# Gate stores from SyncE's queue in quarters, maxima in quarters, and two idle buffers for the first expert table

## The chip, the core and the metric

One core of one Trainium2 chip runs the whole program. The metric is the device time of one execution in microseconds (us). TensorE (PE) does the matmuls, VectorE (DVE) and ScalarE (ACT) the elementwise work, GpSimd (POOL) issues the gathers that go by an index list, and SyncE (SP) issues the plain loads. DMAs can be issued by SP, ACT and POOL, each on a queue of its own.

## The reference, cut to what matters

Two transformer blocks in float32 run one after the other on 256 tokens of width 2048. The change lies in the last part of the first block, a mixture over 16,384 experts, of which each token takes 16 in each of 8 heads:

```python
def peer(x, w_pq, sub_k1, sub_k2, u_emb, v_emb):     # T = 256 tokens, D = 2048
    q = (xt @ w_pq).reshape(T, 8, 2, 128)
    s1, s2 = ...                                     # scores against 2 x 128 keys per head
    v1, i1 = lax.top_k(s1, 16); v2, i2 = lax.top_k(s2, 16)
    cand = v1[..., :, None] + v2[..., None, :]       # 256 pairs, expert = i1 * 128 + i2
    sc, sel = lax.top_k(cand, 16)
    gates = jax.nn.softmax(sc, axis=-1)
    act = jax.nn.gelu(xt . u_emb[expert])            # first expert table, 128 MB
    return sum over experts of gate * act * v_emb[expert]   # second expert table
```

## The kernel before, in words

**Dense first table.** The kernel doesn't gather rows of `u_emb`. It computes the activation of every token with every expert as a dense product (stage u, line 777 on): 32 column blocks, each of four weight tiles of 128x2048 floats (1 MB), so 128 tiles. Stage v (line 798 on) then takes only those rows of `v_emb` that some token uses.

**A weight tile.** `linear` (138) calls `wtile` (108): SP loads a tile into `raw`, a pool of three buffers (112), line 113. `halves` (116) cuts it in two halves of 1024 columns; for each, ACT rounds the values into `whi` (123) and DVE subtracts to get the rest, `wlo` (124). Each of these has four buffers of half a tile. PE multiplies three times for each 128x512 piece: high by high (134), high by low (135), low by high (136), in all 24 matmuls of 512 columns for a tile. A tile's buffer is free for the next load when DVE has made the second `wlo` of it.

**Block end of stage u.** ACT applies gelu (783), PE transposes (790), ACT copies to `actT` (792), and ACT's queue stores it to the DRAM array AG (794).

**Routing beside it.** At a lower priority the scheduler puts the routing between the work of stage u. The gates (lines 651 to 682) come in four sets of 64 tokens. For each token a one-hot matmul (667) gives its gates for all 128x128 experts. ACT copies the high part out (672), and DVE adds the low part and puts the sum into `gsb` (673), an array of 128x128x64 floats of which there is one buffer. At the end of a set, ACT's queue stores `gsb` to AG in two halves of 2 MB (676), and DVE takes the maximum over the 64 tokens in one instruction (678 for even sets, 681 for odd ones). After the fourth set, lines 684 to 774 find out which experts are used, and build lists of them: sixteen groups of three DVE instructions (743, 745, 749) and eight matmuls (752), which end in `idv` (758) and `idg` (762). With `idv` POOL gathers rows of `v_emb` (130, into `raw` and `vraw`), with `idg` it gathers gates and activations from AG (130, into `vag`); `vh` (824) is their product, `vhh` and `vhl` (826, 828) its two parts, and stage v multiplies them by the rows.

**Order.** The tile framework's scheduler writes the order on each engine ahead of time, by priorities and its own simulated timeline. An instruction on an engine, and a DMA in an engine's queue, does not start before the ones that stand ahead of it there.

Of the kernel before, what the change touches and what calls it, by code (L numbers as in the profile page):

```python
# [12 lines left out]
F32 = mybir.dt.float32  # L13
# [5 lines left out]
ALU = mybir.AluOpType  # L19
AX = mybir.AxisListType  # L20

P = 128
# [34 lines left out]
def tile_kernel(ctx: ExitStack, tc: tile.TileContext, A, out):  # L57
    nc = tc.nc
    V, S, G, TE = nc.vector, nc.scalar, nc.gpsimd, nc.tensor

    def pool(name, bufs=1, space=None, stack=ctx):
        kw = {"space": space} if space is not None else {}
        return stack.enter_context(tc.tile_pool(name=name, bufs=bufs, **kw))
# [8 lines left out]
    def bank(name="bk"):  # L72
        tg, nb = {"lin": ("lin", 3), "tp": ("tp", 2), "sc": ("sc", 2), "z": ("sc", 2)}.get(name, ("x", 1))
        return pp.tile([P, 512], F32, tag=tg, name=name, bufs=nb)
# [29 lines left out]
    def wtile(src, step=2048, rows=None, raw=None):  # L104


        if raw is None:
            raw = wp.tile([P, 2048], F32, tag="raw", name="raw", bufs=3)
        if rows is not None:
            gather(raw, src, rows)  # L110
        else:
            for c in range(0, 2048, step):
                nc.sync.dma_start(raw[:, c:c + step], src[:, c:c + step])
        return halves(raw, min(step, 1024))

    def halves(raw, step):
        hi, lo = [], []
        for e in range(2):
            h = wp.tile([P, 1024], F32R, tag="whi", name="whi", bufs=WB)
            l = wp.tile([P, 1024], F32R, tag="wlo", name="wlo", bufs=WB)  # L120
            for c in range(0, 1024, step):
                r, q = raw[:, e * 1024 + c:e * 1024 + c + step], slice(c, c + step)
                S.activation(h[:, q], r, AF.Copy)  # L123
                V.tensor_sub(l[:, q], r, h[:, q].bitcast(F32))  # L124
            hi += [h[:, 0:512], h[:, 512:1024]]
            lo += [l[:, 0:512], l[:, 512:1024]]
        return hi, lo

    def gather(dst, src, rows):
        G.indirect_dma_start(out=dst, out_offset=None, in_=src,  # L130
                             in_offset=bass.IndirectOffsetOnAxis(ap=rows, axis=0))

    def mm3(ps, xh, xl, wh, wl, start, stop):
        TE.matmul(ps, lhsT=xh, rhs=wh, start=start, stop=False)  # L134
        TE.matmul(ps, lhsT=xh, rhs=wl, start=False, stop=False)  # L135
        TE.matmul(ps, lhsT=xl, rhs=wh, start=False, stop=stop)  # L136

    def linear(w, n, xt, kts, kbase=0, before=None):

        ps = [bank("lin"), bank("lin")]  # L140
        for kt in kts:
            if before is not None:
                before(kt)
            wh, wl = wtile(w[n, kt], 512 if before is not None and kt == kts[0] else 2048)
            for e, tt in ((0, 0), (0, 1), (1, 0), (1, 1)):
                for k in (2 * e, 2 * e + 1):
                    xh, xl = xt(4 * (kt - kbase) + k)
                    t = slice(tt * P, (tt + 1) * P)
                    mm3(ps[tt], xh[:, t], xl[:, t], wh[k], wl[k],
                        kt == kts[0] and k == 0, kt == kts[-1] and k == 3)  # L150
        return ps
# [89 lines left out]
    stp = pool("st1", 6, stack=s1)  # L241
# [7 lines left out]
    xt = St(stp, 16, "xt")  # L249
# [105 lines left out]
    for c in range(2):  # L355
        lru_half(c, linear(WIN, c, xt, range(4), before=load_x if c == 0 else None))
# [4 lines left out]
    for c in range(2):  # L361
        ps = linear(WIN, 2 + c, xt, range(4))
# [6 lines left out]
        for j in range(0, 4, 2):  # L369
# [9 lines left out]
            for jj in range(2):  # L379
                xh, xl = yl(4 * c + j + jj)  # L380
                split(y[:, jj, :], xh, xl, vcol("g_lru", 4 * c + j + jj))
                for tt in range(2):
# [4 lines left out]
                        axis=AX.X, op=ALU.add)  # L387
# [6 lines left out]
    ps = linear(WIN, 4, xt, range(4))  # L394
# [77 lines left out]
    for c in range(2):  # L472
        ps = linear(WIN, 5 + c, xt, range(4))
# [35 lines left out]
    x1t = St(stp, 16, "x1t")  # L509
# [17 lines left out]
    AGv = AG.rearrange("(i p) (e a t) -> p i e a t", p=P, e=2, a=2)  # L527
# [22 lines left out]
    for n in range(4):  # L550
        ps = linear(A["w_pq"], n, x1t, range(4))
# [13 lines left out]
        for tt in range(2):  # L565
            ps = bank("sc")
# [10 lines left out]
    @contextmanager  # L577
    def prompt():

        low[0] = tc.cur_priority  # L580
        tc.cur_priority = low0
        yield
        tc.cur_priority = low[0]
# [9 lines left out]
    for tt in range(2):  # L593
# [23 lines left out]
        for half, op, c in ((0, ALU.logical_shift_right, 4), (1, ALU.bitwise_and, 15)):  # L617
# [5 lines left out]
            for h in range(8):  # L623
# [4 lines left out]
                                op=ALU.mult)  # L628
                V.tensor_reduce(kf[:, h, :], eq, axis=AX.X, op=ALU.add)
            dec.append(kf)  # L630
        ps = bank("sc")
# [12 lines left out]
    gp = pool("gates", 1, stack=r3p)  # L644


    used = rp.tile([P, 2, P], F32, tag="used", name="used")
# [3 lines left out]
    for c in range(4):  # L651
        gsb = gp.tile([P, P, 64], F32, tag="gsb", name="gsb", bufs=1)
        for t0 in range(0, 64, 4):
            t = 64 * c + t0
            io = iota.unsqueeze(1).to_broadcast([P, 4, P])
            oh = gp.tile([P, 4, P], F32R, tag="oh2", name="oh2", bufs=2)
            V.tensor_tensor(oh, io, i2T[:, t:t + 4].unsqueeze(2).to_broadcast([P, 4, P]), op=ALU.is_equal)
            o1 = gp.tile([P, 4, P], F32, tag="oh1", name="oh1", bufs=2)
            V.tensor_tensor(o1, io, i1T[:, t:t + 4].unsqueeze(2).to_broadcast([P, 4, P]), op=ALU.is_equal)
            og = gp.tile([P, 4, 2, P], F32R, tag="og", name="og", bufs=2)  # L660
            V.tensor_tensor(og[:, :, 1, :], o1, gT[:, t:t + 4].unsqueeze(2).to_broadcast([P, 4, P]), op=ALU.mult)
            for k0 in range(0, 4, 2):
                ps = bank("sc")
                for k in range(k0, k0 + 2):
                    with prompt():
                        S.activation(og[:, k, 0, :], o1[:, k, :], AF.Copy, scale=gTh[:, t + k:t + k + 1])
                        TE.matmul(ps[:, (k - k0) * T:(k - k0 + 1) * T], lhsT=oh[:, k, :],
                                  rhs=og[:, k].rearrange("p a b -> p (a b)"), start=True, stop=True)
                pv = ps.rearrange("p (k m i) -> p m i k", k=2, m=2)
                gh = gp.tile([P, P, 2], F32, tag="gh", name="gh", bufs=2)  # L670
                with prompt():
                    S.activation(gh, pv[:, 0], AF.Copy)
                    V.tensor_tensor(gsb[:, :, t0 + k0:t0 + k0 + 2], gh, pv[:, 1], op=ALU.add)
        h, t0 = c // 2, c % 2 * 64
        for e in range(0, P, 64):
            S.dma_start(AGv[:, 1 + e:65 + e, h, 1, t0:t0 + 64], gsb[:, e:e + 64, :])
        if t0 == 0:
            V.tensor_reduce(used[:, h, :], gsb, axis=AX.X, op=ALU.max)
        else:
            um = gp.tile([P, P], F32, tag="um", name="um")  # L680
            V.tensor_reduce(um, gsb, axis=AX.X, op=ALU.max)
            V.tensor_tensor(used[:, h, :], used[:, h, :], um, op=ALU.max)
    r3p.close()

# [86 lines left out]
    ps = bank("sc")  # L771
# [3 lines left out]
    r1p.close()  # L775
    tc.cur_priority = low0

    for n in range(32):
        ps = linear(A["u"], n, x1t, range(4))
        act = []  # L780
        for tt in range(2):
            a = up.tile([P, 512], F32, tag="act", name="act", bufs=2)
            S.activation(a, ps[tt], AF.Gelu_apprx_tanh, scale=r1[:, tt:tt + 1])
            act.append(a)
        aT = up.tile([P, 4, T], F32, tag="actT", name="actT", bufs=2)
        for j in range(0, 4, 2):
            tp = bank("tp")
            for jj in range(2):
                for tt in range(2):
                    TE.transpose(tp[:, jj * T + tt * P:jj * T + (tt + 1) * P],  # L790
                                 act[tt][:, (j + jj) * P:(j + jj + 1) * P], ident)
            S.activation(aT[:, j:j + 2, :], tp.rearrange("p (a t) -> p a t", a=2), AF.Copy)
        for tt in range(2):
            S.dma_start(AGv[:, 4 * n + 1:4 * n + 5, tt, 0, :], aT[:, :, tt * P:(tt + 1) * P])
# [4 lines left out]
    stp = pool("st2", 8, stack=s2)  # L799
# [65 lines left out]
    for i, b in enumerate(order):  # L865
# [5 lines left out]
        raw = vp.tile([P, 2048], F32, tag="vraw", name="vraw", bufs=2) if i % 5 in (1, 3) else None  # L871
# [7 lines left out]
    with tc.If(more > 0):  # L879
        with tc.For_i(0, P, 1) as k:  # L880
# [8 lines left out]
            raw = wp.tile([P, 2048], F32, tag="raw", name="raw", bufs=3)  # L889
            nc.sync.dma_start(raw, VE[bass.ds(k * P, P), :])  # L890
            for c in range(4):
# [5 lines left out]
                for tt in range(2):  # L897
# [5 lines left out]
                    op=ALU.mult)  # L903
# [97 lines left out]
    for c in range(2):  # L1001
        ps = linear(W2, 4 + c, y1t, range(4))
# [3 lines left out]
    for h0 in (0, 4):  # L1006
        for tt in range(2):
            s = mq.tile([P, 4, T], F32, tag="s2", name="s2", bufs=2)
            for j in range(2):
                bias = mq.tile([P, 2, T], F32, tag="bias", name="bias", bufs=1)  # L1010
                nc.sync.dma_start(bias, A["bias"][tt, :, h0 + 2 * j:h0 + 2 * j + 2, :])
                ps = bank("sc")
                for hh in range(2):
                    h = h0 + 2 * j + hh
# [35 lines left out]
    for j in range(16):  # L1050
        xh, xl = y1t(j)
        c = slice(j % 4 * P, (j % 4 + 1) * P)
        wh, wl = kh[j // 4][:, c], kl[j // 4][:, c]
# [32 lines left out]
    for c in range(2):  # L1086
        ps = linear(A["w_ukv"], 2 + c, ckvt, range(1))
# [7 lines left out]
    for h0 in (0, 4):  # L1095
        for tt in range(2):
# [4 lines left out]
            for e in range(2):  # L1101
                ps = bank("sc")
                b = slice(64 * e, 64 * e + 64)
                for j in range(2):
                    h = h0 + 2 * j + e
# [50 lines left out]
    for lo_, hi_ in ((0, 6), (6, 11)):  # L1156
# [21 lines left out]
        for n in range(4):  # L1178
            ps = linear(A["w_dn"], n, at.__getitem__, range(lo_, hi_))
# [98 lines left out]
```

## Time and profile before

| | |
|---|---|
| three runs, us | 3049.87, 3050.18, 3055.47; median 3050.18 |
| profiled execution, us | 3049.11, of which the span of the trace is 3047.3 |
| mean granted TensorE clock of it | 0.990 of full speed |
| busy share of the span | PE 97%, DVE 66%, ACT 52%, POOL 9% |
| read from HBM, written to it | 583.77 MB, 40.11 MB |

The span is cut here by events of stage u: its blocks run from 450 to 1256 us, the gates' four sets end at 698, 829, 960 and 1087 us, and stage v starts at 1271 us. A set's end is the moment at which DVE begins its maximum; the prediction calls it R. An idle time in brackets at the end of a row is the time for which the engine stood still ahead of the row, with what released it. "issue" is a wait for the engine's own instruction stream. PEclk and "granted clock" say which share of TensorE's full speed it had.

### The profile page before, as it was taken

Reading aid. Unit: us, or ns where it says so; the run is one execution under the profiler, and the core shown is the slowest. Engines: PE = TensorE matmul, PEld = TensorE weight load, DVE = VectorE, ACT = ScalarE, POOL = GpSimd, SP = SyncE. Lnnn points to the kernel's source line nnn. Section 1 sums busy time; section 2 is a strip of 40 time slices with the busy share of each in tenths; the row PEclk is TensorE's granted clock in tenths of the full one; section 3 lists DMA queues with packets and bytes.
Section 4 is the critical chain, followed back from the end, with each engine's and each line's share of the span. In section 5 each row is a group of like instructions: output and inputs, shape, how many; then the busy total and the mean of one; then the engine's idle time right before and its main releaser. Section 6 shows DMA issues by size and latency. Waiting matters only on the chain. (4 is left out here: it accounts for less than half of the span.)

```text
span 3047.3 us, 36250 instructions
## 1 busy us (share of the span) xinstructions
PE 2970.9 (97%) x13729; PEld 2443.6 (80%) x13729; DVE 2002.0 (66%) x2944; ACT 1576.9 (52%) x2221; POOL 271.0 (9%) x232
## 2 busy tenths in 40 slices
PE   9999999998988999899999999999999999999999
PEld 7887888887877778678887788778888888888887
DVE  6885789877766769467777756664655454445454
ACT  6754545565655645455565555544444444344443
POOL 0000000000000000477662000000000000000000
PEclk9999999999999999999999999999999999999999
DMA  6442546656567575688886454554655555555554
GB/s 231 155 174 98 180 166 210 215 196 219 189 205 217 181 232 184 226 327 325 333 322 250 173 183 169 205 179 169 242 193 187 194 185 188 193 193 194 190 190 159
DMA packets 197168, 626.26 MB, mean 206 GB/s; under 512 B 82688, under 2 KB 116096, under 8 KB 129664
## 3 DMA queue, kind: packets, MB, share of 16 engines
q1 hardware_dynamic: 73728, 460.55, 42.8%
q0 software_dynamic: 20784, 124.79, 11.1%
q10 hardware_dynamic: 102480, 38.58, 4.8%
q8 instruction: 108, 1.77, 0.2%
q14 instruction: 68, 0.56, 0.1%
HBM read 583.77 MB, written 40.11 MB: 205 GB/s over the span
## 5 line engine op out<-in xcount | busy, mean ns | idle before, releaser
L124 DVE TENSOR_TENSOR wlo<-raw,whi 128x1024 fp32r<-128x1024 f32 (+1 forms) x972 | 1181.4, 1221 | 772.5 <-ACT whi L123 759.8
L123 ACT ACTIVATE whi<-raw 128x1024 fp32r<-128x1024 f32 (+1 forms) x972 | 1023.4, 1057 | 1087.0 <-PE lin L136 901.6
L134 PE MATMUL lin<-whi,x1th 128*128 128x512 f32 x1152 | 451.5, 399 | 25.4 <-ACT whi L123 25.4
L135 PE MATMUL lin<-wlo,x1th 128*128 128x512 f32 x1152 | 457.9, 397 | 6.2 <-DVE wlo L124 6.2
L136 PE MATMUL lin<-whi,x1tl 128*128 128x512 f32 x1152 | 457.1, 397 | 0.0
L134 PEld LDWEIGHTS lin<-whi,x1th 128*128 128x128 f32 x1152 | 219.6, 191 | 70.0 <-ACT whi L123 27.7
L136 PE MATMUL lin<-whi,x3tl 128*128 128x512 f32 x704 | 274.9, 391 | 0.0
L135 PE MATMUL lin<-wlo,x3th 128*128 128x512 f32 x704 | 274.2, 389 | 0.0
L134 PE MATMUL lin<-whi,x3th 128*128 128x512 f32 x704 | 269.5, 390 | 0.0
L135 PEld LDWEIGHTS lin<-wlo,x1th 128*128 128x128 f32 x1152 | 220.4, 191 | 51.3 <-DVE wlo L124 8.5
L136 PEld LDWEIGHTS lin<-whi,x1tl 128*128 128x128 f32 x1152 | 220.1, 191 | 43.5
L135 PE MATMUL lin<-wlo,y1th 128*128 128x512 f32 x512 | 200.7, 393 | 0.8 <-DVE wlo L124 0.8
L134 PE MATMUL lin<-whi,y1th 128*128 128x512 f32 x512 | 199.4, 395 | 1.7 <-ACT y1th L159 1.2
L136 PE MATMUL lin<-whi,y1tl 128*128 128x512 f32 x512 | 198.5, 393 | 0.8 <-DVE y1tl L160 0.8
L135 PEld LDWEIGHTS lin<-wlo,x3th 128*128 128x128 f32 x704 | 132.2, 188 | 27.3
L136 PEld LDWEIGHTS lin<-whi,x3tl 128*128 128x128 f32 x704 | 132.2, 188 | 27.1
L134 PEld LDWEIGHTS lin<-whi,x3th 128*128 128x128 f32 x704 | 132.2, 188 | 26.9
L130 POOL DMA_INDIRECT vag<-ag,idg x102 | 134.2, 1315 | 53.7 <-issue 26.5
L136 PE MATMUL lin<-whi,at 128*128 128x512 f32 x352 | 137.2, 390 | 0.0
L135 PE MATMUL lin<-wlo,at 128*128 128x512 f32 x352 | 137.0, 389 | 0.0
L134 PE MATMUL lin<-whi,at 128*128 128x512 f32 x352 | 135.5, 389 | 0.0
L134 PEld LDWEIGHTS lin<-whi,y1th 128*128 128x128 f32 x512 | 96.2, 188 | 22.4 <-ACT y1th L159 1.8
(440 smaller groups left out, 4750.1 us busy)
## 6 DMA issues: line engine op xcount, KB each, us to landing
raw<-in_u_dram SPq DMA_DIRECT2D x128, 1024.0 KB, 4.8
raw<-in_w_in_dram SPq DMA_DIRECT2D x91, 1024.0 KB, 4.8
raw<-in_w_gu_dram SPq DMA_DIRECT2D x88, 1024.0 KB, 4.8
raw<-in_w_dn_dram SPq DMA_DIRECT2D x44, 1024.0 KB, 4.7
raw<-in_w_out_dram SPq DMA_DIRECT2D x16, 1024.0 KB, 4.8
raw<-in_w_pq_dram SPq DMA_DIRECT2D x16, 1024.0 KB, 4.8
ag<-actT ACTq DMA_DIRECT2D x64, 256.0 KB, 3.0
ag<-gsb ACTq DMA_DIRECT2D x8, 2048.0 KB, 15.5
```

The source lines that it names most:

```text
L123: S.activation(h[:, q], r, AF.Copy)
L124: V.tensor_sub(l[:, q], r, h[:, q].bitcast(F32))
L130: G.indirect_dma_start(out=dst, out_offset=None, in_=src, in_offset=bass.IndirectOffsetOnAxis(ap=rows, axis=0))
L134: TE.matmul(ps, lhsT=xh, rhs=wh, start=start, stop=False)
L135: TE.matmul(ps, lhsT=xh, rhs=wl, start=False, stop=False)
L136: TE.matmul(ps, lhsT=xl, rhs=wh, start=False, stop=stop)
```

## The change

SP issues the stores of a set in place of ACT, as four of 1 MB each in place of two of 2 MB. The one maximum becomes four, each over a quarter of the experts, into `um`, which is then copied or combined into `used`. And two buffers of the pool "st1", which hold an earlier activation and are idle by then, take the weight tiles with an odd number in stage u; those with an even number keep the three of `raw`.

```diff
@@ -135,13 +135,14 @@
         TE.matmul(ps, lhsT=xh, rhs=wl, start=False, stop=False)
         TE.matmul(ps, lhsT=xl, rhs=wh, start=False, stop=stop)
 
-    def linear(w, n, xt, kts, kbase=0, before=None):
+    def linear(w, n, xt, kts, kbase=0, before=None, raws=None):
 
         ps = [bank("lin"), bank("lin")]
         for kt in kts:
             if before is not None:
                 before(kt)
-            wh, wl = wtile(w[n, kt], 512 if before is not None and kt == kts[0] else 2048)
+            wh, wl = wtile(w[n, kt], 512 if before is not None and kt == kts[0] else 2048,
+                           raw=raws and raws(kt))
             for e, tt in ((0, 0), (0, 1), (1, 0), (1, 1)):
                 for k in (2 * e, 2 * e + 1):
                     xh, xl = xt(4 * (kt - kbase) + k)
@@ -672,13 +673,13 @@
                     S.activation(gh, pv[:, 0], AF.Copy)
                     V.tensor_tensor(gsb[:, :, t0 + k0:t0 + k0 + 2], gh, pv[:, 1], op=ALU.add)
         h, t0 = c // 2, c % 2 * 64
-        for e in range(0, P, 64):
-            S.dma_start(AGv[:, 1 + e:65 + e, h, 1, t0:t0 + 64], gsb[:, e:e + 64, :])
+        um = gp.tile([P, P], F32, tag="um", name="um")
+        for e in range(0, P, 32):
+            nc.sync.dma_start(AGv[:, 1 + e:33 + e, h, 1, t0:t0 + 64], gsb[:, e:e + 32, :])
+            V.tensor_reduce(um[:, e:e + 32], gsb[:, e:e + 32, :], axis=AX.X, op=ALU.max)
         if t0 == 0:
-            V.tensor_reduce(used[:, h, :], gsb, axis=AX.X, op=ALU.max)
+            V.tensor_copy(used[:, h, :], um)
         else:
-            um = gp.tile([P, P], F32, tag="um", name="um")
-            V.tensor_reduce(um, gsb, axis=AX.X, op=ALU.max)
             V.tensor_tensor(used[:, h, :], used[:, h, :], um, op=ALU.max)
     r3p.close()
 
@@ -775,8 +776,10 @@
     r1p.close()
     tc.cur_priority = low0
 
+
+    ur = [stp.tile([P, 2048], F32, tag="st", name="uraw") for _ in range(2)]
     for n in range(32):
-        ps = linear(A["u"], n, x1t, range(4))
+        ps = linear(A["u"], n, x1t, range(4), raws=lambda kt: ur[kt // 2] if kt % 2 else None)
         act = []
         for tt in range(2):
             a = up.tile([P, 512], F32, tag="act", name="act", bufs=2)
```

Lines behind the edits carry higher numbers in the kernel after: 673 becomes 674, 743 becomes 744, 794 becomes 797.

On ACT this stood at the end of the first set (`whi` of two stage u halves, the gate's copies, the two stores, the next block's gelu):

```order
L672 ACTIVATE gh<-sc 128x256
L666 ACTIVATE og<-oh_4494,gTh 128x128 x4
L123 ACTIVATE whi<-raw 128x1024
L672 ACTIVATE gh<-sc 128x256
L676 DMA ag<-gsb 128x64x64 x2
L123 ACTIVATE whi<-raw 128x1024 x2
L672 ACTIVATE gh<-sc 128x256
L666 ACTIVATE og<-oh_4516,gTh 128x128 x4
L123 ACTIVATE whi<-raw 128x1024 x2
L783 ACTIVATE act<-lin,r_2876 128x512 x2
```

The stores are gone from ACT. On SP this now stands at the same place, where before there was nothing but loads into `raw`:

```order
L113 DMA uraw<-in_u_dram 128x2048
L113 DMA raw<-in_u_dram 128x2048
L113 DMA uraw<-in_u_dram 128x2048
L113 DMA raw<-in_u_dram 128x2048
L113 DMA uraw<-in_u_dram 128x2048
L113 DMA raw<-in_u_dram 128x2048
L678 DMA ag<-gsb 128x32x64 x4
L113 DMA uraw<-in_u_dram 128x2048
L113 DMA raw<-in_u_dram 128x2048
L113 DMA uraw<-in_u_dram 128x2048
L113 DMA raw<-in_u_dram 128x2048
```

The four stores stand in the one queue by which the tiles of stage u come, ahead of the next load.

On DVE, the first set ended in this way, with the first add into `gsb` for the second set in the next to last row:

```order
L659 TENSOR_TENSOR oh_4538<-iota,i1T 128x512
L678 TENSOR_REDUCE used<-gsb 128x128
L124 TENSOR_TENSOR wlo<-raw,whi 128x1024 x2
L657 TENSOR_TENSOR oh_4514<-iota,i2T 128x512
L661 TENSOR_TENSOR og<-oh_4516,gT 128x4x128
L124 TENSOR_TENSOR wlo<-raw,whi 128x1024 x2
L659 TENSOR_TENSOR oh_4560<-iota,i1T 128x512
L124 TENSOR_TENSOR wlo<-raw,whi 128x1024 x2
L673 TENSOR_TENSOR gsb<-gh,sc 128x128x2 x2
L657 TENSOR_TENSOR oh_4536<-iota,i2T 128x512
```

and now it ends in this way, with that add in the next to last row again:

```order
L679 TENSOR_REDUCE um<-gsb 128x32 x4
L124 TENSOR_TENSOR wlo<-uraw,whi 128x1024 x2
L658 TENSOR_TENSOR oh_4521<-iota,i2T 128x512
L662 TENSOR_TENSOR og<-oh_4523,gT 128x4x128
L124 TENSOR_TENSOR wlo<-raw,whi 128x1024 x2
L681 COPY used<-um 128x128
L660 TENSOR_TENSOR oh_4567<-iota,i1T 128x512
L124 TENSOR_TENSOR wlo<-uraw,whi 128x1024 x2
L124 TENSOR_TENSOR wlo<-raw,whi 128x1024 x2
L674 TENSOR_TENSOR gsb<-gh,sc 128x128x2 x2
L124 TENSOR_TENSOR wlo<-uraw,whi 128x1024 x2
```

The four maxima stand directly behind each other, and the first add of the next set has eight halves of `wlo` between itself and them, where there were six.

At the end of stage u, DVE had the last list instructions, and then `ids` to `idg`, ahead of twelve further halves of `wlo`:

```order
L743 TENSOR_TENSOR ln<-iota,lb 128x1024
L749 TENSOR_TENSOR bb_5820<-b_5818,iota_5549 128x808
L124 TENSOR_TENSOR wlo<-raw,whi 128x1024 x2
L754 COPY ids<-x 128x202
L756 SCALAR_TENSOR_TENSOR idf<-ids 128x101
L124 TENSOR_TENSOR wlo<-raw,whi 128x1024
L757 TENSOR_SCALAR ids<-idf 128x101
L758 CAST idv<-ids 128x101
L760 TENSOR_SCALAR idf<-idf 128x59
L761 TENSOR_SCALAR idf<-idf 128x30
L762 CAST idg<-idf 128x101
L124 TENSOR_TENSOR wlo<-raw,whi 128x1024 x12
```

Now the last four groups of the list stand behind the last `wlo` of stage u (a row `wlo<-uraw,whi 128x1024 x2`, eight rows ahead of the first one here), and the next `wlo` after `idg` is stage v's own:

```order
L744 TENSOR_TENSOR ln<-iota,lb 128x1024
L750 TENSOR_TENSOR bb_5829<-b_5827,iota_5573 128x808
L744 TENSOR_TENSOR ln<-iota,lb 128x1024
L750 TENSOR_TENSOR bb_5844<-b_5842,iota_5573 128x808
L755 COPY ids<-x 128x202
L757 SCALAR_TENSOR_TENSOR idf<-ids 128x101
L758 TENSOR_SCALAR ids<-idf 128x101
L759 CAST idv<-ids 128x101
L761 TENSOR_SCALAR idf<-idf 128x59
L762 TENSOR_SCALAR idf<-idf 128x30
L763 CAST idg<-idf 128x101
L124 TENSOR_TENSOR wlo<-raw,whi 128x1024 x2
```

On POOL, the gathers began with seven of rows for stage v:

```order
L130 DMA vraw<-in_v_dram,idv 128x2048 x2
L130 DMA raw<-in_v_dram,idv 128x2048 x4
L130 DMA vraw<-in_v_dram,idv 128x2048
L130 DMA vag<-ag,idg 128x256 x4
L130 DMA vag<-ag,idg 128x512 x2
L130 DMA vag<-ag,idg 128x256 x5
```

and now begin with three, ten of gates and activations, and then two more:

```order
L130 DMA raw<-in_v_dram,idv 128x2048 x3
L130 DMA vag<-ag,idg 128x256 x4
L130 DMA vag<-ag,idg 128x512 x2
L130 DMA vag<-ag,idg 128x256 x4
L130 DMA vraw<-in_v_dram,idv 128x2048 x2
L130 DMA raw<-in_v_dram,idv 128x2048
```

So the gathers into `vraw`, the second and the fourth tile of stage v, have moved behind the first ten of `vag`.

## Rows read from the trace of the kernel before

**Rows 1.** Page part 1: busy us, share of the span, instructions.

```profile
PE 2970.9 (97%) x13729; PEld 2443.6 (80%) x13729; DVE 2002.0 (66%) x2944; ACT 1576.9 (52%) x2221; POOL 271.0 (9%) x232
```

**Rows 2.** Windows: length, busy us (instructions) by engine, PEclk, DMA.

```profile
473.41:660.11 186.70, 186.70 (x877) 155.13 (x876) 165.80 (x369) 108.51 (x169) 0.53 (x1) 1.00 0.60 205
660.11:1130.04 469.93, 432.25 (x1985) 356.00 (x1984) 331.53 (x414) 270.13 (x519) 0.00 (x0) 0.96 0.65 208
1130.04:1255.69 125.65, 125.65 (x650) 103.36 (x649) 100.89 (x118) 67.86 (x77) 6.22 (x6) 1.00 0.59 212
```

**Rows 3.** Waits of PE, 660 to 1130 us: total, times, longest.

```profile
PE lin L134 <- ACT whi L123: 25.4, 6, 7.6
PE lin L135 <- DVE wlo L124: 6.2, 5, 1.7
PE sc L667 <- DVE gsb L673: 5.9, 4, 1.7
```

**Rows 4.** Timeline of ACT, sets 1, 3: start, us, row [idle <-releaser].

```profile
697.95 9.98 ACTq L676 DMA_DIRECT2D ag<-gsb  x1
707.97 2.00 ACT L123 ACTIVATE whi<-raw 128x1024 fp32r<-128x1024 f32 x2 [9.97 <-issue]
984.11 2.00 ACT L123 ACTIVATE whi<-raw 128x1024 fp32r<-128x1024 f32 x2 [10.16 <-issue]
```

**Rows 5.** Timeline of DVE, first and second set.

```profile
698.03 8.68 DVE L678 TENSOR_REDUCE used<-gsb 128x128 f32<-128x8192 f32 x1
726.59 0.75 DVE L673 TENSOR_TENSOR gsb<-gh,sc 128x256 f32<-128x256 f32 x2 [6.54 <-DMA ag<-gsb]
858.23 0.76 DVE L673 TENSOR_TENSOR gsb<-gh,sc 128x256 f32<-128x256 f32 x2 [6.75 <-DMA ag<-gsb]
```

**Rows 6.** Timeline of PE, first and third set.

```profile
710.03 0.69 PE L134 MATMUL lin<-whi,x1th 128*128 128x512 f32 x1 [5.01 <-ACT whi L123]
970.43 0.50 PE L135 MATMUL lin<-wlo,x1th 128*128 128x512 f32 x1 [1.26 <-DVE wlo L124]
```

**Rows 7.** Tile gsb: landing of its stores.

```profile
DMA to landing us min/median/max: 11.2/15.5/28.6
```

**Rows 8.** DMA by queue, 690 to 740 us: packets, MB, engine share.

```profile
q10 hardware_dynamic: 18528, 5.24, 44.8%
q1 hardware_dynamic: 872, 6.36, 34.3%
```

**Rows 9.** Line 113, 660 to 1130 us: landing of the u loads.

```profile
DMA to landing us min/median/max: 4.6/4.8/8.4
```

**Rows 10.** Timeline of PE and DVE, 1216 to 1222 us.

```profile
1217.51 0.88 PE L752 MATMUL x<-bb,ln 128*128 128x202 bf16 x8
1218.43 0.37 DVE L754 COPY ids<-x 128x202 f32<-128x202 f32 x1 [1.36 <-PE x L752]
1220.61 0.22 DVE L758 CAST idv<-ids 128x101 uint32<-128x101 f32 x1
```

**Rows 11.** Timeline of POOL, 1222 to 1264 us.

```profile
1222.48 1.55 POOL L130 DMA_INDIRECT vraw<-in_v_dram,idv  x1 [641.19 <-ACT whi L123]
1224.33 0.94 POOL L130 DMA_INDIRECT vraw<-in_v_dram,idv  x1 [0.30 <-issue]
1263.23 0.95 POOL L130 DMA_INDIRECT vag<-ag,idg  x1 [2.08 <-DMA ag<-actT]
```

**Rows 12.** Timeline of PE, end of u and start of v.

```profile
1257.79 0.88 PE L790 MATMUL tp<-ident,act 128*128 128x128 f32 x6 [0.56 <-ACT act L783]
1271.34 0.80 PE L134 MATMUL tp<-whi,vhh 128*128 128x512 f32 x1 [12.67 <-ACT vhh L826]
```

**Rows 13.** DMA issues, 1220 to 1320 us: count, median us to landing.

```profile
vraw<-in_v_dram,idv POOLq DMA_INDIRECT x6, 8.9
```

**Rows 14.** Groups on DVE, 660 to 1256 us: busy us, mean ns.

```profile
L743 DVE TENSOR_TENSOR ln<-iota,lb 128x1024 bf16<-128x1024 f32 x16 | 19.5, 1221 | 1.2 <-PE x L752 1.1
L749 DVE TENSOR_TENSOR bb<-b,iota 128x808 bf16<-128x808 bf16 x16 | 15.9, 995 | 0.0
```

## The prediction

> **What bounds the kernel now.** I read the page's first part, then windows, then the waits of PE, and then the timelines of ACT, DVE and PE where PE stood still. PE is busy for 97% of the span [rows 1], so time can be won only where it idles or runs at the lower of its two clock levels (1.2 against 2.4 GHz). The windows show where that is. From 473 to 660 us, eight blocks of stage u, PE never stops and has its full clock: 23.3 us a block, 5.8 a tile, 2.9 a half tile. The same from 1130 to 1256 us. Between them, in the 17 blocks in which the four sets of gates end, it is busy for 432.25 of 469.93 us, so 37.7 us are idle, and the mean granted clock is 0.96, which is another 0.04 x 470 = 18.8 us [rows 2]. Together 56.5 us are lost there; each idle us brings another half by the clock.
>
> Three waits make up 37.5 of the 37.7 us: 25.4 for `whi` of ACT, 6.2 for `wlo` of DVE, 5.9 for gates that DVE hadn't added into `gsb` [rows 3]. The timelines explain them. At R (698.03 in the first set) ACT sits inside the issue of its second store for 9.98 us, and does no `whi` until 707.97; in the third set there is a like hole of 10.16 us, behind the next stores in its queue [rows 4]. At the same time DVE does the maximum for 8.68 us, and some 20 us later its first add for the next set waits 6.54 and 6.75 us for the stores to have read the one `gsb` [rows 5]. PE lives on what is split ahead: in the first set it ran out at 710.03 - 5.01 = 705.0, R + 7 [rows 6].
>
> **The change part by part.**
>
> *Stores off ACT.* The wait of 25.4 us goes as far as it is ACT's. Late next is DVE: the four maxima stand directly behind each other in the order, so they hold DVE for what one did, 8.7 us, whatever the diff suggests. DVE is then free at R + 8.7, its first `wlo` is there at about R + 10, and PE without ACT's hole has the high-by-high products of the next halves to do first. So a stall of at most 3.1 us remains (R + 10.1 against R + 7); the third set shows the low end, where `whi` was ready and PE waited 1.26 us for `wlo` [rows 6]. Four sets: 5 to 12 us. I take 7, near the row of 1.26 with some of the clock added. The copy of `um` and three more starts of a maximum cost DVE under 1 us a set, beside that.
>
> *Stores in the queue of the loads.* SP does nothing else than issue, so the time of issuing costs it nothing by itself; what is behind the stores there is the next load. The stores' own time: from 690 to 740 us, ACT's queue moved 18,528 packets in 44.8% of 16 x 50 us, 19.3 ns each [rows 8]. The four stores are 4.19 MB in runs of 256 bytes, 16,384 packets, 1,024 an engine: 19.8 us when nothing else runs, and up to 28.6 us as now, beside loads of the other queue (from 697.95 [rows 4] to the end of the wait at 726.59 [rows 5], which is the longest landing of [rows 7]). I take R + 22, nearer to the time alone, since in the order the loads now stand behind them in the same queue. Two things want that end:
>
> - The first add of the next set. It stands eight halves behind the maxima and no longer six, so two halves, 5.8 us, later than R + 22 (726.59 less the wait of 6.54): at R + 28, or R + 26 where less stall lies in between. It waits nothing by my value, and 1 to 3 us a set by the long one.
> - The next tile. Before, three buffers held the tiles ahead, now five do. PE has splits until R + 7, and five tiles of 5.8 us last until R + 36; with the split, the sixth must have landed by about R + 31. A load takes 4.8 us, at most 8.4 beside the stores now [rows 9]: R + 27 to R + 31 by my value, R + 34 to R + 37 by the long one, which is 3 to 6 us of stall a set; if the queue lets a load pass, as two queues do now, it lands long before and the cover is whole.
>
> Now loads go on while the other queue's stores are on their way, and none took over 8.4 us [rows 9]. The Trainium skill (page "DMA: Bandwidth & Descriptors", section "Queues, rings and completion order") says that a DMA engine takes turns between the queues that have work, and takes the descriptors of one queue in order; the row of 8.4 us agrees with the first half, and no run here shows the second yet. By that rule the loads lose their turns, as I have it; without it they would keep landing in some 8 us, and the sum would be the same, since my value leaves no stall either way. The Trainium skill (page "Perfetto Trace Analysis", section "DMA Optimizations") also advises giving loads to one issuing engine and stores to another: by that this edit goes the wrong way, and the time would be that of the slower rival below.
>
> *Two more buffers* add no instruction; they are the cover just counted, and with three the sixth tile would be the fourth, needed 11.6 us earlier, a stall of 7 to 11 us a set.
>
> The region gives back 56.5 - 7 = 49.5 us (bounds: 56.5 - 3, and 56.5 - 12 - 4 x 6 = 20).
>
> *The end of stage u.* Counted in DVE's order, the fourth set's maxima stand behind 340 halves of `wlo` where it was 326, seven tiles later, so the list is late: its last four groups stand behind the last `wlo` of stage u. Before, `idv` was done at 1220.8, the first two gathers of rows were issued from 1222.48 on [rows 10, 11], and with 8.9 us to land [rows 13] had long come when PE ended stage u at E = 1257.79 - 0.56 = 1257.2. The restart hung on the gathers of `vag` alone: first issue at 1263.23, E + 6.0 [rows 11], PE at 1271.34, E + 14.1 [rows 12]. Now two list groups remain for PE and DVE after E: 0.9 us of matmuls, 2 x (1.22 + 0.99) us on DVE [rows 14], another 0.9 of matmuls and 1.1 for `ids` to `idv` [rows 10], so `idv` at E + 7.3. The first gather goes 1.65 us later, as before (1222.48 against 1220.83), and three gathers of rows take 4.3 us ahead of the first of `vag` (1.55, then 0.94 and 0.30 of gap each): E + 13.3. From there to PE it was 8.1 us; with three tiles in flight ahead I put 9. Restart at E + 22, so 8 us later than before. Then the second tile: its gather comes after ten of `vag`, E + 13.3 + 10 x 1.25 = E + 25.8, lands 8.9 us later [rows 13], and is split at E + 36; the first tile keeps PE to about E + 28. Another 8 us. Sum 16; least 5 (if the lists get ahead of the order's end as I read it, and only the three gathers count), most 28 (if both waits are longer by half, and the tiles after them too). Nothing hides this: PE has no other work then.
>
> *Sum.* 3049.1 (the profiled execution) - 49.5 + 16 = 3015.6. The median of the runs lies 1.1 above that execution: 3017.
>
> **The rivals.** A difference of 0.2%, 6 us, is about the least that can be told from no change here.
>
> 1. *The end is nearly free.* `idv` is ready in time after all, and the late gathers are covered. For it: DVE was busy for only 100.89 of the last 125.65 us [rows 2], and can run ahead of PE. Against: the order has the list behind the last half, and its matmuls behind PE's last of stage u. Loss 3 in place of 16: 3004.
> 2. *DVE keeps the stall.* The maxima hold PE for the full 3.1 us a set and the clock falls with it, so that 4 x 5 = 20 remain; the rest as forecast: 3049.1 - 36.5 + 20 = 3033. For it: 8.7 us on DVE against 7 us of splits. Against: the 1.26 us of [rows 6]. "Maxima by quarters" then does not do what it says.
> 3. *Loads starve behind the stores: slower.* Place: the load of the sixth tile after R. If four stores need 33 us or more, it lands at R + 38, 7 us late, and with half as much by the clock a set loses 10 us, 40 in all; with 16 at the end that is all of 56.5, and from there on the kernel is slower. At 36 us it is 10 us late: 4 x 10 x 1.5 = 60, with 16 at the end less 56.5, so 3069. For it: 28.6 us were seen. Against: that was beside loads, 6.36 MB in those 50 us [rows 8], and the stores alone come to 19.8.
>
> **How the numbers follow.** Forecast 0.57, first rival 0.15, second 0.18, third 0.06; 0.04 lies between the second and the third, at no change. Faster by over 0.2%: 0.57 + 0.15 + 0.18 = 0.90, the same 0.04, slower 0.06. The range runs from 2998 (the first rival with the smallest rest, 3049 - 53 + 2) to 3040 (the second with an end of 27).
>
> **What the profile after would show.** Right: no idle of about 10 us on ACT after R; PE waits of 1 to 3 us for `wlo` at the four ends; no wait of `gsb` adds for a store; mean clock of the gate blocks at 0.99 or more; a gap of about 22 us on PE behind stage u, with a second of some 8 us after one tile. Wrong: a wait of `whi` for a load into `raw` or `uraw` in the 40 us after an R (third rival), waits for `wlo` of 3 us and more with the clock at half (second), or a first gather ahead of E (first).

## The result and the profile after

The changed kernel takes 3016.14 us (median of four runs, 3012.49 to 3017.87) against 3052.26 us for the kernel before (four runs). The ratio is 0.9886, 95% interval 0.9873 to 0.9898: 36 us faster. Its profiled execution took 3017.87 us, span 3016.0, the slowest of its four; against the span of 3047.3 before, the two traces to compare differ by 31.3 us.

The page's first part of the changed kernel, to be read beside [rows 1]:

```profile
PE 2958.9 (98%) x13729; PEld 2437.0 (81%) x13729; DVE 2005.1 (66%) x2958; ACT 1578.3 (52%) x2221; POOL 270.7 (9%) x232
```

PE does the same 13,729 matmuls with 12 us less of busy time (most of it by the clock, which is higher) and 19 us less of idle time. Where? Cut the span at E, the end of stage u on PE: 1257.23 us before, and now 1210.65. Windows of the kernel before, up to E and behind it (length, busy us by engine, PEclk, DMA):

```profile
660.11:1257.23 597.12, 559.44 (x2641) 460.39 (x2639) 433.37 (x530) 338.86 (x597) 6.22 (x6) 0.97 0.64 208
1257.23:1400.00 142.77, 127.05 (x547) 103.66 (x547) 93.33 (x94) 74.10 (x82) 103.06 (x80) 0.95 0.78 284
```

and of the changed kernel, cut at the same events:

```profile
659.87:1210.65 550.78, 541.85 (x2609) 449.34 (x2608) 425.99 (x530) 335.12 (x591) 0.00 (x0) 0.99 0.65 210
1210.65:1400.00 189.35, 165.94 (x734) 136.25 (x733) 128.82 (x133) 99.93 (x108) 133.37 (x103) 0.93 0.84 314
```

Up to E the changed kernel is 597.12 - 550.78 = 46.3 us faster. From E to the end of the span it takes 1805.4 us, where it took 1790.1: 15.3 lost. With 0.2 us won ahead of the first window that is the 31.3 between the spans.

What the 46.3 are: PE idled 597.12 - 559.44 = 37.7 us up to E, and now 8.9. The lower clock cost 15.9 us there, and now costs 3.4 (PE's busy time in each window of 1 us, times what its PEclk lacks to 1; idle time is left out, since it is counted already). So the gates lose 12.3 us in place of 53.6. Up to 3.5 us of the rest are work that only moved: four groups of list matmuls, 0.88 us each, which PE now does behind E. Behind E, to 1400 us, idle time went from 15.7 to 23.4 us and the clock's part from 2.7 to 4.4.

The waits of PE in the changed kernel, 640 to 1300 us (total, times, longest), answer to [rows 3]:

```profile
PE tp L134 <- ACT vhh L829: 19.0, 1, 19.0
PE lin L135 <- DVE wlo L124: 8.5, 5, 2.8
PE tp L134 <- ACT whi L123: 2.6, 1, 2.6
PE x L753 <- DVE bb L750: 1.8, 2, 1.2
PE lin L134 <- ACT whi L123: 0.4, 1, 0.4
```

The 25.4 us for `whi` of ACT have shrunk to 0.4, the 5.9 for `gsb` are gone, and the waits for `wlo` grew from 6.2 to 8.5. On PE's timeline they stand singly at the four set ends; the last two rows are the start of stage v (compare [rows 6, 12]):

```profile
707.74 0.50 PE L135 MATMUL lin<-wlo,x1th 128*128 128x512 f32 x1 [2.73 <-DVE wlo L124]
841.04 0.50 PE L135 MATMUL lin<-wlo,x1th 128*128 128x512 f32 x1 [1.04 <-DVE wlo L124]
969.66 0.50 PE L135 MATMUL lin<-wlo,x1th 128*128 128x512 f32 x1 [1.44 <-DVE wlo L124]
1097.95 0.80 PE L135 MATMUL lin<-wlo,x1th 128*128 128x512 f32 x1 [2.75 <-DVE wlo L124]
1235.55 0.79 PE L134 MATMUL tp<-whi,vhh 128*128 128x512 f32 x1 [19.03 <-ACT vhh L829]
1243.59 0.73 PE L134 MATMUL tp<-whi,vhh 128*128 128x512 f32 x2 [2.56 <-ACT whi L123]
```

ACT, at the same set end, no longer stands in an issue. It is out of work until PE has used up an earlier half:

```profile
704.36 1.06 ACT L123 ACTIVATE whi<-raw 128x1024 fp32r<-128x1024 f32 x1 [0.48 <-PE lin L136]
711.48 1.06 ACT L123 ACTIVATE whi<-uraw 128x1024 fp32r<-128x1024 f32 x1 [6.06 <-PE lin L136]
```

The timeline of SP at the first set end, R = 697.7, shows the four stores and the load behind them, and the landing of that load stands below:

```profile
697.24 15.25 SPq L678 DMA_DIRECT2D ag<-gsb  x4
712.58 4.95 SPq L113 DMA_DIRECT2D uraw<-in_u_dram  x1
```

```profile
DMA to landing us min/median/max: 11.0/11.0/11.0
```

SP is inside the four issues for 15.25 us, as ACT was inside its second one before; but SP has nothing to do but issue. The load behind them, issued at R + 15, landed 11.0 us later, R + 26, in place of the 4.8 us of [rows 9]; in the other three sets also at R + 26. In each set it landed after the last of the four stores, by 2.8 to 4.2 us. In the kernel before, a load issued at R + 12.3 on a queue without stores landed at R + 20.3, ahead of a store of ACT's queue that took until R + 28.5. So the loads do stand behind the stores of their queue here. This agrees with the Trainium skill (page "DMA: Bandwidth & Descriptors", section "Queues, rings and completion order"), by which an engine takes the descriptors of one queue in order. PE did not have to wait for this load.

DVE at the third set end, and its end of the lists and start of stage v:

```profile
959.62 8.86 DVE L679 TENSOR_REDUCE um<-gsb 128x32 f32<-128x2048 f32 x4
982.27 0.76 DVE L674 TENSOR_TENSOR gsb<-gh,sc 128x256 f32<-128x256 f32 x2 [2.25 <-DMA ag<-gsb]
1217.51 0.21 DVE L759 CAST idv<-ids 128x101 uint32<-128x101 f32 x1
1234.08 0.69 DVE L827 TENSOR_TENSOR vh<-vag 128x512 f32<-128x512 f32 x1 [3.24 <-DMA vag<-ag,idg]
```

The four maxima are one row of 8.86 us, against 8.68 for one maximum [rows 5]. The first add of the next set waited for the stores once, until R + 22.65, and not in the other sets. POOL's first gather of rows, its first of `vag`, and its first into `vraw`:

```profile
1218.63 1.09 POOL L130 DMA_INDIRECT raw<-in_v_dram,idv  x1 [637.58 <-DVE idg L763]
1222.51 0.95 POOL L130 DMA_INDIRECT vag<-ag,idg  x1 [0.31 <-issue]
1236.38 1.38 POOL L130 DMA_INDIRECT vraw<-in_v_dram,idv  x1 [0.30 <-issue]
```

`idv` came at E + 7.1, the first gather at E + 8.0, the first of `vag` at E + 11.9; before, they were ahead of E or at E + 6.0 [rows 11].

### The profile page after: what moved, and what is told of

It is laid out like the page before. It is cut to its first block, busy times and chain, and to the rows that moved or that the text cites. A ratio compares the mean times of both kernels' runs of the same rounds, so it can differ in the third digit from the quotient of the medians.

```text
span 3016.0 us, 36313 instructions
## 1 busy us (share of the span) xinstructions
PE 2958.9 (98%) x13729; PEld 2437.0 (81%) x13729; DVE 2005.1 (66%) x2958; ACT 1578.3 (52%) x2221; POOL 270.7 (9%) x232
## 5 line engine op out<-in xcount | busy, mean ns | idle before, releaser
L124 DVE TENSOR_TENSOR wlo<-raw,whi 128x1024 fp32r<-128x1024 f32 (+1 forms) x844 | 1026.5, 1221 | 705.2 <-ACT whi L123 683.9
L123 ACT ACTIVATE whi<-raw 128x1024 fp32r<-128x1024 f32 (+1 forms) x844 | 889.6, 1058 | 960.3 <-PE lin L136 823.8
L124 DVE TENSOR_TENSOR wlo<-uraw,whi 128x1024 fp32r<-128x1024 f32 x128 | 155.8, 1221 | 51.6 <-ACT whi L123 50.9
L123 ACT ACTIVATE whi<-uraw 128x1024 fp32r<-128x1024 f32 x128 | 135.2, 1058 | 103.7 <-PE lin L136 101.4
L130 POOL DMA_INDIRECT raw<-in_v_dram,idv x61 | 80.2, 1315 | 684.9 <-DVE idg L763 637.6
L136 PE MATMUL lin<-whi,at 128*128 128x512 f32 x352 | 137.2, 390 | 0.0
```

Source lines behind the costliest of these rows:

```text
L130: G.indirect_dma_start(out=dst, out_offset=None, in_=src, in_offset=bass.IndirectOffsetOnAxis(ap=rows, axis=0))
```

## The experiments

My theory was that the gain comes from taking the stores off ACT, that the two buffers only shield the loads behind the stores and cost the late lists, and that the maxima in quarters do nothing. Rival A says that the deeper prefetch of stage u is the gain; rival B, the maxima in quarters. The first four runs undo or do one part alone.

**Without the two buffers.** `linear(A["u"], n, x1t, range(4))` again, the rest as changed.

> The changed kernel without the two extra buffers: stores on SyncE in quarters, maxima in quarters, three buffers for stage u. Its order ends the lists as early as the kernel before (all behind half 366 and not 376). My theory (the gain is the stores' leaving ACT; the two buffers only cover the loads that stand behind the stores, and are what makes the lists late): the loss of 15 us at the start of stage v is gone, but PE waits for whi behind a late load of stage u, 5 to 8 us a set, with the clock some 36 us for four sets: about 3037 us (3020 to 3050). Rival A (the gain is the deeper prefetch of stage u): about 3050. Rival B (the gain is the maxima in quarters, the buffers do nothing for it): about 3001.

Measured: 3027.2 us (3021.5 to 3030.3), ratio to before 0.9915 [0.9898, 0.9931]. Its PE waits, 640 to 1300 us:

```profile
PE tp L134 <- ACT vhh L828: 12.7, 1, 12.7
PE lin L135 <- DVE wlo L124: 12.1, 8, 2.9
PE sc L668 <- DVE gsb L674: 5.9, 4, 1.7
PE lin L134 <- ACT whi L123: 1.4, 3, 0.7
```

24 us of the gain are there without the buffers, so A falls, and B's 3001 as well. But my price was wrong too: PE waits for `whi` only 1.4 us in all. The load behind the stores landed at the same R + 26, and three buffers were just enough: ACT began to split that tile at R + 31.8, 28.1, 28.5 and, in the fourth set, at 25.9, as soon as it had landed. I read this as the need having moved back, by PE's remaining stall at R and the gates' own matmuls; it was not tried by itself. What is lost instead is the old wait for `gsb`, 5.9 us as before, and 12.1 for `wlo`: in this order the first add stands six halves behind the maxima again. The start of stage v is the old one (12.7).

**Stores by ACT again.**

```diff
-            nc.sync.dma_start(AGv[:, 1 + e:33 + e, h, 1, t0:t0 + 64], gsb[:, e:e + 32, :])
+            S.dma_start(AGv[:, 1 + e:33 + e, h, 1, t0:t0 + 64], gsb[:, e:e + 32, :])
```

> The changed kernel with its four stores a set issued by ACT again, the two buffers and the maxima in quarters kept. My theory: ACT sits in the issue of stores for some 10 us at each R again, PE waits for whi 5 to 7 us a set and more with the clock, the late lists stay: about 3055 us (3045 to 3065), that is no faster than the kernel before. Rival A (prefetch) and rival B (maxima in quarters): 3016 to 3020, since both of their causes are still in it.

Measured: 3051.1 us (3050.0 to 3052.8), ratio 1.000 [0.9991, 1.0010]. Waits of PE, 640 to 1300 us:

```profile
PE lin L134 <- ACT whi L123: 22.4, 3, 10.6
PE tp L134 <- ACT vhh L829: 18.9, 1, 18.9
PE tp L793 <- ACT act L786: 9.0, 1, 9.0
```

With both of the rivals' causes kept, the whole gain is gone: the wait for ACT is back at 22.4 us, 9.0 more stand before the transposes that need ACT's gelu, and the late start of stage v stays. Of the 33.0 us between this profile and that of the changed kernel, 29.5 lie ahead of E.

**One maximum.** The four reduces replaced by `V.tensor_reduce(um, gsb, axis=AX.X, op=ALU.max)`.

> The changed kernel with one maximum over all experts a set, as before, in place of four quarters. My theory: the four stand back to back on DVE (8.86 us) and cost what one costs (8.68), so 3016 us (3012 to 3020), waits for wlo of 1 to 3 us at each R as they are. Rival B: the stall of DVE comes back in full, 3030 to 3040. Rival A: 3016.

Measured: 3018.0 us (3014.6 to 3023.0), ratio 0.9896 [0.9879, 0.9912]; waits of PE:

```profile
PE lin L135 <- DVE wlo L124: 6.7, 4, 2.7
PE tp L134 <- ACT vhh L829: 18.9, 1, 18.9
```

The same as the changed kernel, with 6.7 us for `wlo` where that has 8.5. So the quarters are worth nothing in the sum; B falls. The parts are not the same: in this order E comes 6.1 us sooner (1204.5), and the lists later (`idv` at E + 14.1, restart at E + 31.8).

**The two buffers alone**, in the kernel before.

> The kernel before with the two extra buffers alone. My theory: the stall by ACT stays, the wait for the stores' landing shrinks because the first add of the next set stands two halves later, and the lists come late (behind half 376), some 15 us at the start of stage v: 3055 us (3045 to 3065), not faster than before. Rival A: about 3017 to 3025. Rival B: 3050, no change.

Measured: 3045.0 us (3042.5 to 3048.5), ratio 0.9981 [0.9971, 0.9991]: at the low edge of what I gave, and 6 us faster than before, where I had said not faster. It is far from rival A's 3017 to 3025. Waits of PE:

```profile
PE lin L134 <- ACT whi L123: 12.8, 3, 7.0
PE tp L134 <- ACT vhh L829: 18.9, 1, 18.9
PE tp L793 <- ACT act L786: 10.0, 3, 5.2
```

The wait for `gsb` is gone. That for ACT has only moved: 12.8 us for `whi` and 9.6 of the 10.0 for the gelu stand in the four sets, together 22.4, where 25.4 were before. Ahead of its E (1227.1) this kernel is some 30 us faster than the one before, work that moved behind E included, and behind it 25 us slower: PE restarts at E + 36.3. So the late lists belong to the buffers: they come with them here, and go with them in the first run.

The two parts side by side: the buffers alone gave 6 us, SP's stores alone 24, both together 36. So the buffers do more than shield: with the stores off ACT they are worth another 12 us, even after what the late lists cost.

**Lists earlier.** The constants `tri`, `trib`, `iota1`, `pidx` are made ahead of the gates, and ACT multiplies:

```diff
-        V.tensor_tensor(bb[:, 1], b1, bc(iota1, j, NL), op=ALU.mult)
+        for i in range(J):
+            S.activation(bb[:, 1, i], b1[:, i], AF.Copy, scale=float(j + i + 1))
```

> The changed kernel with the lists made earlier: the two small constants that the lists need are loaded before the gates, not after the last set, and ACT in place of DVE multiplies each list block (750) by its number. In its order idv stands behind half 372 and not 376, and the gathers of the second and fourth tile of stage v again ahead of those of vag. My theory (15 us are lost between stages u and v because the lists end behind stage u): the first gather goes ahead of E, PE restarts at E + 14 to 17, no second gap: 3003 us (2998 to 3010). Rival (what is lost there is something else, say DMA contention of the gathers): 3012 to 3017.

Measured: 3011.3 us (3006.6 to 3012.3), ratio 0.9866 [0.9850, 0.9883]. PE behind stage u:

```profile
1214.94 1.45 PE L794 MATMUL tp<-ident,act 128*128 128x128 f32 x8 [0.25 <-ACT act L787]
1230.78 0.80 PE L134 MATMUL tp<-whi,vhh 128*128 128x512 f32 x1 [14.39 <-ACT vhh L830]
```

The mechanism is as expected: PE restarts at E (1214.7) + 16.1, and the second gap shrinks, though to 1.6 us and not to nothing. The size is outside what I gave. E itself is 4.1 us later than in the changed kernel, and the list matmuls that stood behind E (four groups of 0.88 us, 3.5 at most) are ahead of it now; the rest of the 4.1 I did not trace. That work never was a loss, and I had counted it as one.

**Maxima by tokens.** After every 16 tokens of a set, a maximum over those 16 goes into `used`, so that only a quarter is left at R.

> The changed kernel with maxima over 16 tokens each, three of the four of a set made while the set is still being filled, so that DVE is held at R for 2.2 us and not 8.9. My theory (what remains at R are 8 us of waiting for wlo and 5 by the clock): these 13 us go, but stage u then ends sooner against the lists (first list instruction behind half 365 and not 358), which costs some 5 to 10 us at the start of stage v: 3010 us (3004 to 3016), no wait for wlo over 0.5 us at an R. Rival (the residue is the stores' DMA traffic): 3016 or more, the waits stay.

Measured: 3024.8 us (3023.7 to 3026.5), ratio 0.9914 [0.9897, 0.9931]: slower than the changed kernel, outside what I gave. Waits of PE:

```profile
PE tp L134 <- ACT vhh L828: 18.9, 1, 18.9
PE x L752 <- DVE bb L749: 9.1, 5, 4.1
PE sc L668 <- DVE gsb L674: 3.4, 2, 1.7
PE lin L134 <- ACT whi L123: 2.2, 2, 1.2
```

No wait for `wlo` is left, so the cause of the residue is right. But two waits for `gsb` with 2.2 us for `whi` behind them took their place some 30 us after R, with a drop of the clock at both (6.1 us by it on PE's busy time up to E, 3.4 in the changed kernel), so E comes only 3.7 us sooner. And the lists are later still: five waits for `bb` on PE, `idv` at E + 20, restart at E + 38.

**Both, with three list arrays in memory of their own.**

> Maxima by tokens, the earlier lists, and the first three arrays of the lists in memory of their own, so that they need not wait for the last stores of gsb. In its order idv stands behind half 375. My theory: the 13 us at the four R go and PE restarts at E + 14 to 18 with no second gap: 2993 us (2986 to 3002), faster than both kernels. Rival (DMA traffic at both places): 3010 to 3017.

Measured: 3019.1 us (3015.2 to 3019.8), ratio 0.9896 [0.9880, 0.9913]. The same as the changed kernel; my 2993 was wrong, as the run before had shown half of already: what the maxima by tokens save at R they lose at the next adds. And although `idv` is there 11 us ahead of E, stage v starts late: two gathers of rows that stand ahead of the first of `vag` waited 6.3 and 6.5 us for a free buffer, so that one went at E + 12.6 and PE restarted at E + 20.8.

**Stores twice.** Behind each store a second one of the same quarter, to an array that nothing reads.

> The changed kernel with every store of gsb issued a second time, to a DRAM array that nothing reads. Doubles the suspected cost: the first load behind the stores landed at R + 26 in the changed kernel, so it lands at about R + 45 here. My theory (loads of one queue stand behind its stores; five buffers last to R + 31 to 36): PE waits for whi 8 to 14 us a set, half as much again by the clock, 50 to 85 us in all: 3080 us (3060 to 3105), and ACT waits for the DMA of raw or uraw. Rival (loads pass stores): 3010 to 3025, since the lists are a little earlier in its order.

Measured: 3091.9 us (3089.4 to 3093.8), ratio 1.0134 [1.0117, 1.0150]. Waits of PE, 640 to 1340 us, and SP in the first set (the first of eight stores, and the load behind them):

```profile
PE sc L670 <- DVE gsb L676: 30.0, 9, 9.6
PE lin L134 <- ACT whi L123: 19.4, 3, 17.2
PE lin L135 <- DVE wlo L124: 8.3, 5, 2.8
```

```profile
698.08 0.41 SPq L680 DMA_DIRECT2D ag<-gsb  x1
734.89 4.70 SPq L113 DMA_DIRECT2D uraw<-in_u_dram  x1
```

The time is as expected and the rival (loads pass stores) falls: the load was issued at R + 36 and landed 9.6 us later, R + 46. But in three sets the wait that came first was another: 30.0 us for `gsb`, whose one buffer the stores still read. Of the 19.4 for `whi`, 17.2 stand in one piece in the fourth set, where no add follows. There ACT waits for the load itself:

```profile
1170.68 2.00 ACT L123 ACTIVATE whi<-uraw 128x1024 fp32r<-128x1024 f32 x2 [25.71 <-DMA uraw<-in_u_dram]
```

The slower case of the prediction exists, at double the stores; in the fourth set it is the load, as I had it, and in the others it begins at the add.

**The changed kernel again, and lists earlier still**, side by side. The second is the fifth run's kernel, with `m3`, `mb` and `colsum` of the lists in memory of their own.

> The changed kernel itself, unaltered, beside the next one on the same chip, since the runs so far leave it open whether earlier lists gain anything over it. 3016 us (3012 to 3018).

> The changed kernel with the earlier lists of the run before (constants loaded ahead of the gates, the block multiplied by ACT), and the first three arrays of the lists in memory of their own, so that they need not wait for the last stores of gsb; maxima as in the changed kernel. In its order the first list instruction stands behind half 350 and idv behind 371 (changed kernel: 358 and 376; kernel before: 341 and 366). My theory (the lists being late costs E + 25 to the restart in place of E + 14 to 16, of which 3.5 us are list matmuls that move ahead of E): restart at E + 14 to 16.5, no second gap over 1 us, 3009 us (3005 to 3013), 5 to 9 us under the changed kernel of this call. Rival (nothing is won by earlier lists, the difference seen was noise between calls): equal to the changed kernel within 2 us.

Measured: 3013.4 us (3012.1 to 3016.2), ratio 0.9882 [0.9866, 0.9899], for the changed kernel, and 3008.1 us (3006.2 to 3012.2), ratio 0.9864 [0.9847, 0.9880], for the other. 5.4 us between the medians is what I gave, but the intervals overlap, so this says "likely" and not more. The traces say it more firmly. PE at E = 1215.25 and at its restart, and DVE's `idv`:

```profile
1216.03 0.88 PE L795 MATMUL tp<-ident,act 128*128 128x128 f32 x6 [0.56 <-ACT act L788]
1229.63 0.80 PE L134 MATMUL tp<-whi,vhh 128*128 128x512 f32 x1 [12.73 <-ACT vhh L831]
```

```profile
1192.23 0.22 DVE L761 CAST idv<-ids 128x101 uint32<-128x101 f32 x1
```

`idv` is ready 23 us ahead of E, and PE restarts at E + 14.4, the old distance [rows 12]. Against the profile of the changed kernel taken beside it, E is 6.5 us later and the way from E to the end 10.4 us shorter. This is the fastest kernel here.

## Why the prediction was right

**Stores off ACT: right, the rest mis-sized.** Predicted 49.5 us won in the region, measured 46.3 up to E, with up to 3.5 of moved work in it. I left 7 us, and 12.3 are left: waits for `wlo` of 2.73, 1.04, 1.44 and 2.75 us, 1.0 of others, and 3.4 by the clock. I took the value near the 1.26 of [rows 6]; two sets of four were near the other bound of 3.1. The 56.5 was too large as well: its 18.8 for the clock count the low clock also while PE stood still, which is in the 37.7 already. On PE's busy time it is 15.9, so 53.6 were lost. That ACT was the cause is shown by the second experiment, where putting it back takes all of the gain away, and that the quarters are not, by the third.

**Stores in the loads' queue: right.** The stores let the first add go at R + 22.65, where I had put R + 22; it waited in one set of four. PE's only other waits in that set, 1.0 us some 8 us later, may come from it or not. The load behind landed at R + 26 against R + 27 to R + 31, in another way than I had worked out: SP issued it at R + 15 and it took 11 us, where I had let it start after the stores and take 4.8 to 8.4.

**What the two buffers are for: wrong.** I said that with three of them PE would stall for 7 to 11 us a set. The first experiment has 1.4 us in all. The step that failed is the need: I had the tile wanted landed by R + 19, and it landed at R + 26 in time. I counted from R + 7 with tiles of 5.8 us and some 5 us for the split, and left out that PE stops for 2.9 us at R and runs slower behind it; that this makes up the difference is my reading, and no run tries it. What the buffers gave was another thing, by way of the order: the first add two halves later, clear of the stores.

**The end of stage u: right in the sum, by errors that cancel.** Predicted 16 us, measured 15.3, and 11.4 in the second profile of the same kernel (the ninth run). The gathers were where I had put them: `idv` at E + 7.1 (E + 7.3), the first of `vag` at E + 11.9 (E + 13.3), the second tile's at E + 25.7 (E + 25.8). From the first of `vag` to PE it was 13.0 us and not 9, with three gathers of 1 MB ahead of it, so the restart came at E + 24.9 and not E + 22. The second gap was 2.56 us and not 8: PE had restarted later, and ACT had the second tile 6.1 us after its gather, not 8.9. Not in the sum at all were the up to 3.5 us of list matmuls which had only moved, and the clock: 1.7 us more on PE's busy time up to 1400 us, and 3.2 in two falls near 1640 and 1672 us that the second profile doesn't have. The fifth and tenth experiments show the part that can be had back, some 5 us and not 15. So the mechanisms of the two large terms were right, and that the forecast of 3017 came within 1 us of the median is luck.

**The rivals.** The first (the end is nearly free) falls on the first gather at E + 8.0. The second (DVE keeps the stall) is true of two sets in four. The third (loads starve) did not come; it was seen only with twice the stores, and there in one set of four.

## What to carry to other kernels

A large store of small pieces can hold the engine that issues it, here ACT for 10 us and SP for 15: give it to an engine that has no computing in its stream (only SP was tried here), even if that puts it ahead of loads, and check the landing of the first load behind it against what PE still has in hand. When a change speeds up one stream, look in the order at what was scheduled beside it: low-priority work that used to fit may now end behind the stage it was hidden under. And before a gap is counted as a loss, subtract the work that only moved into it.

## What the runs showed of the hardware that was not expected

- After the same wait of PE the clock did not always do the same. In the changed kernel's first profile it fell behind both waits of 2.7 us (0.88 and 0.77 from 705 to 710 and from 710 to 715 us in the first set), in its second profile only behind that of the first set (2.67 us), in the fifth and tenth experiments only behind that of the fourth, while 2.82 us in the first left it at 1.00. Behind waits of 1.0 and 1.4 us it stayed at 1.00 each time. So some 1.7 us a set end come and go from run to run with no change in the kernel.
- Issuing goes at the pace of the stores: of the four of 1 MB in the first set, the first took SP 0.4 us to issue and the others 4.5 to 5.5 us each, and they landed 4.8 to 5.2 us apart. With eight stores the load behind them was issued 36.8 us after the first.
- From POOL's first gather of `vag` to PE's restart it was 12.9 to 13.0 us in each kernel where three gathers of rows were issued just ahead of it (the changed one in both profiles, and the second, third, fourth and sixth experiments), and 8.1 to 8.2 us in each where they were not (the kernel before, and the first, fifth, seventh, eighth and tenth).
